# Two buffers for four tiles of a decoder's delta-rule stage, one scaling moved a stage earlier, and a smaller DMA scratch

## The chip, the core and the metric

The kernel runs on one NeuronCore of a Trainium2 chip. Its engines are named as in the profile: PE (TensorE, matrix products and transposes; PEld its weight loads), DVE (VectorE), ACT (ScalarE), POOL (GpSimd) and SP, which here only issues DMAs. A matrix product goes from SBUF into PSUM. The metric is device time in microseconds (us) of one launch, and its median over repeated launches.

## The reference, cut to what matters

Two layers of a decoder over 512 tokens of width 1024. Each layer is a half-step SwiGLU, a mixer, a cross-attention and a second half-step. The mixer's projection feeds three groups of heads: forgetting attention (FoX), block-sparse attention (MoBA) and RWKV-7 time mixing. The change touches the last, whose eight heads of 64 each carry a 64 x 64 state through the tokens:

```
def step(state, inp):
    r_t, w_t, k_t, v_t, kk_t, a_t = inp
    sa = einsum('bhij,bhj->bhi', state, -kk_t)
    state = (state * w_t[:, :, None, :] + sa[..., None] * (kk_t * a_t)[:, :, None, :]
             + v_t[..., None] * k_t[:, :, None, :])
    return state, einsum('bhij,bhj->bhi', state, r_t)
```

Everything else is dense projections, softmax attention and norms, in f32.

## The kernel before, in words

The recurrence is not run token by token. The 512 tokens are cut into 8 chunks of 64, and the 8 heads are taken as 4 head pairs (called 0 to 3 here; two heads fill 128 partitions). A pair goes through six stages, each a function (a generator):

- scaled (L620 on): projections r, k, v become tiles scaled with the cumulated decay. ER holds what is multiplied by the decay since the chunk's start, B what is divided by it, and DC (128 x 8 x 1) the decay to each chunk's end (the copy at L665).
- Gram (`rwkv_gram`): products of B and ER for each chunk (L717) are masked by DVE into G and BN (L721). The strictly triangular blocks of G are stored to DRAM (L726), come back as 16 x 16 blocks in A (L730), and POOL inverts them in 30 dependent steps (helper L282, tiles T and P), copies the result (L742) and stores it again (L746); it comes back as the tiles Tf and Pf (L749).
- rows (`rwkv_rows`): ER is transposed (L763), v is centered (L769) into KV, G times KV goes into KX (L779), B is multiplied by DC, and the result is transposed into BN (L788).
- inverse (`rwkv_inverse`): the 16 x 16 inverses grow to 64 x 64 (L809 reads Tf; L818, L826, L835 and L842 follow and read Pf).
- transitions (`rwkv_transitions`): L857 and L871 make the chunk transitions AR.
- states (`rwkv_states`): 8 chunks in sequence. A step adds L900 and L902 in PSUM, and DVE makes the next state as old state times DC plus that (L906). L920 and L924 to L932 norm and gate the output.

Between these small products stand the long ones: three products for each pair of a 128-column block (L152 to L154, and L948 to L950 for values), since an f32 weight is split into a high part (ACT, L145) and a low part (DVE, L146) after its load (SP, L130). Attention units (L1034 to L1046, with softmax on DVE and ACT, L1016 to L1022) belong to the mixer too.

A list of stages (ORDER, with leads in PRI) gives each instruction a priority. The program that builds the kernel then sets the order on each engine from these priorities, its own estimates of times and the number of buffers of each tile name (RW, RP): an instruction that needs a buffer is put in when the tile before it in that buffer has had its last reader. So an order on the engines is fixed before the kernel runs, and each engine works its list strictly in that order. In the list of stages, the scaling of a pair stands ahead of the states of the pair before it (`s1 ... y0`, `s2 ... y1`, `s3 ... y2`), and those states read that pair's DC and KV. SP's DMAs, weights and small stores alike, also stand in one list.

DC, KV, G and KX have one buffer each; ER, BN and six others have two.

Of the kernel before, what the change touches and what calls it, by code (L numbers as in the profile page):

```python
# [11 lines left out]
ALU = mybir.AluOpType  # L12
# [3 lines left out]
P = 128  # L16
# [32 lines left out]
RPW = {"ts": 0, "sp": 1, "acc": 0, "tx": 1, "ty": 1}  # L49
BPW = {"acc": 0, "sp": 2, "pt": 0, "po": 1}  # L50

RW = {"e": 2, "tk1": 2, "tk2": 2, "zr": 2, "zv": 2, "ER": 2, "zk": 2, "BN": 2}
RP = {"acc": 1, "tx": 1, "ty": 2, "ts": 2, "sp": 2}
WP = {"wraw": 3, "whi": 2, "wlo": 2}

# [60 lines left out]
class Trunk:  # L116
# [585 lines left out]
    def rwkv_gram(self, l, hp, st):  # L702

        nc, rw = self.nc, self.rw
        ps = lambda c=8: self.bank(TAGS["g"], c)
        mm = nc.tensor.matmul
        ER, B = st["ER"], st["B"]

        G = st["G"] = rw.tile([P, 16, 64], F32, name="G", tag="G")

        BN = st["BN"] = rw.tile([P, 8, 4, 64], F32, name="BN", tag="BN")
        for q in range(2):
            pg = [ps(4).rearrange("p c (i t) -> p c i t", i=2) for h in range(2)]
            for c in range(4):
                g, i = 2 * q + c // 2, c % 2
                for h in range(2):
                    mm(pg[h][:, c].rearrange("p i t -> p (i t)"), B[H[h], g, 2 * i:2 * i + 2].rearrange("p a b -> p (a b)"),  # L717
                       ER[H[h], g, 1:3] if i == 0 else ER[H[h], g, 0:4:3], start=True, stop=True)
            for h in range(2):
                for i, dst in ((0, G[:, 8 * h + 4 * q:8 * h + 4 * q + 4]), (1, BN[:, 4 * q:4 * q + 4, 1 + h])):  # L720
                    nc.vector.tensor_tensor(dst, pg[h][:, :, i], self.gmask[:, i:i + 1, :].to_broadcast([P, 4, 64]), op=ALU.mult)  # L721
            yield

        scA, scP, scT = (x[hp % 2] for x in (self.scA, self.scP, self.scT))
        for a in range(2):
            nc.sync.dma_start(scA[a].rearrange("j s t -> s j t"), G[H[a], 1 - a::2])  # L726
        A = rw.tile([64, 16, 16], F32, name="A16", tag="A16")
        for q in range(4):
            d = slice(16 * q, 16 * q + 16)
            nc.sync.dma_start(A[d], scA.rearrange("a j s t -> (a j) s t")[:, d, d])  # L730
        I = rw.tile([64, 16, 16], F32, name="P16", tag="P16")
        tmp = rw.tile([64, 16, 16], F32, name="T16", tag="T16")
        If = I.rearrange("p a b -> p (a b)")
        nc.gpsimd.memset(If, 0.0)
        nc.gpsimd.memset(If[:, 0:256:17], 1.0)
        for u in range(15, 0, -1):
            n = 16 - u
            self.tt("sub", tmp[:, 0:u, 0:n], A[:, 0:u, u:u + 1].to_broadcast([64, u, n]),
                    I[:, u:u + 1, u:16].to_broadcast([64, u, n]), ALU.mult)
            self.tt("sub", I[:, 0:u, u:16], I[:, 0:u, u:16], tmp[:, 0:u, 0:n], ALU.subtract)  # L740
        It = rw.tile([64, 16, 16], F32, name="I16", tag="T16")
        nc.gpsimd.tensor_copy(It, I.rearrange("p a b -> p b a"))  # L742
        for name, sc, src in (("Tf", scT, It), ("Pf", scP, I)):
            for q in range(4):
                d = slice(16 * q, 16 * q + 16)
                nc.sync.dma_start(sc.rearrange("a j s t -> (a j) s t")[:, d, d], src[d])  # L746
            st[name] = rw.tile([P, 8, 64], F32, name=name, tag=name)
            for a in range(2):
                nc.sync.dma_start(st[name][H[a]], sc[a].rearrange("j s t -> s j t"))  # L749
        yield  # L750

    def rwkv_rows(self, l, hp, st):

        nc, rw = self.nc, self.rw
        ps = lambda c=8: self.bank(TAGS["r"], c)
        mm, tr = nc.tensor.matmul, nc.tensor.transpose
        ER, B, G, BN, v = (st[n] for n in ("ER", "B", "G", "BN", "V"))

        KX = st["KX"] = rw.tile([P, 8, 2, 64], F32, name="KX", tag="KX")
        KV = st["KV"] = rw.tile([P, 8, 2, 64], F32, name="KV", tag="KV")  # L760
        pk = ps(4)
        for q in range(4):
            tr(pk[:, q, :], ER[:, q, 0:2].rearrange("p a b -> p (a b)"), self.ident)  # L763
        self.cp("kx", KX[:, :, 0, :].rearrange("p (h q) d -> p q h d", h=2), pk.rearrange("p q (h d) -> p q h d", h=2))
        yield

        pv = ps(4)
        for q in range(4):
            mm(pv[:, q, :], v[:, q * P:(q + 1) * P], self.center, start=True, stop=True)  # L769
        for i in range(2):  # L770
            self.cp("kv", KV[H[i], i::2].rearrange("p q h d -> p q (h d)"), pv[H[i]])
        yield

        px = ps()
        for j in range(8):
            for a in range(2):
                h, i = j // 4, 1 - a
                c = 2 * (j % 4) + i
                mm(px[H[a], j, :], G[H[i], 8 * h + c, :], KV[H[i], c, h, :], start=True, stop=True)  # L779
        self.cp("x", KX[:, :, 1, :], px)  # L780
        yield

        B2 = B.rearrange("p q (i a) b -> p (q i) (a b)", i=2)
        self.tt("B2", B2, B2, st["DC"].to_broadcast([P, 8, P]), ALU.mult)
        for q in range(2):
            pk = ps(4)
            for c in range(4):
                tr(pk[:, c, :], B2[:, 4 * q + c], self.ident)  # L788
            self.cp("bt", BN[:, 4 * q:4 * q + 4, 0:4:3], pk.rearrange("p c (h d) -> p c h d", h=2))
            yield  # L790
# [351 lines left out]
    def mixer_and_xattn(self, l):  # L1142
# [14 lines left out]
        with sb("raw") as raw:  # L1157
# [9 lines left out]
            with sb("rw") as rw0, sb("rwm") as rw1, sb("rwl") as rw2, pp("rp") as rp0, pp("rps") as rp1, pp("rpt") as rp2:  # L1167
                rp = self.tp = TagPool((rp0, rp1, rp2), RP, where=RPW)
                self.rw = at = TagPool((rw0, rw1, rw2), RW, where=LATE)
                w = self.ins['mix_w_in'][l]  # L1170
# [186 lines left out]
```

## Time and profile before

| | |
|---|---|
| median of 3 runs | 2575.36 us (2575.05 to 2586.14) |
| profiled execution | 2590.88 us, span 2589.1 us, 1.8 us around it |
| PE busy | 2497.2 us (96%) |
| DVE, ACT, POOL busy | 1346.6, 846.9, 493.0 us |
| granted TensorE clock, mean | 0.974 of full |
| chain that ended last | PE 86%, DVE 6%, POOL 3%, DMA 2%, ACT 2% |

A busy share of 96% says that PE sets the time, in what it does and in the clock at which it does it; the other engines count only where PE waits for them. PE stands at 2.4 GHz (granted clock 1.00) or 1.2 GHz (0.50). In the timeline rows a bracket gives the idle time of that engine just ahead of the instruction and what ended it.

### The profile page before, as it was taken

What the parts mean: (1) busy time and instruction counts of PE and PEld (TensorE: products, weight loads), DVE (VectorE), ACT (ScalarE), POOL (GpSimd) and SP (SyncE); (2) the same over time, 40 slices, a digit from 0 to 9 for tenths busy, and PEclk for the clock granted to TensorE, in tenths of its full rate; (3) what the DMA queues carried; (4) which work ended last, traced back from release to release, by engine and by line L of the source; (5) the groups of instructions that cost most, each with busy time, mean ns of one, the idle gap of its engine ahead of it and who ended that gap; (6) DMA issues with size and microseconds to landing.
All of it is one profiled execution on the core that took longest, in us unless ns stands there. A gap on an engine that the chain in (4) does not pass through costs nothing.

```text
span 2589.1 us, 35163 instructions
## 1 busy us (share of the span) xinstructions
PE 2497.2 (96%) x13976; PEld 2025.7 (78%) x13976; DVE 1346.6 (52%) x2503; ACT 846.9 (33%) x1337; POOL 493.0 (19%) x610
## 2 busy tenths in 40 slices
PE   8999998899999899999999999999999899999999
PEld 7888876787667788888888888767877677888887
DVE  6444445666755654344444444465666666543444
ACT  4222233233343342222332222333333433422222
POOL 4212120232210122020221211202322110221211
PEclk9999999998889999999999999999978999999999
DMA  4333342221213133333333333422212121333332
GB/s 143 104 98 94 96 130 69 66 59 43 64 34 92 53 96 90 104 93 98 95 94 100 94 98 94 121 75 58 67 34 56 56 78 45 110 98 98 95 95 88
DMA packets 434880, 218.41 MB, mean 84 GB/s; under 512 B 63856, under 2 KB 428828, under 8 KB 434716
## 3 DMA queue, kind: packets, MB, share of 16 engines
q1 hardware_dynamic: 431948, 212.36, 28.9%
q10 hardware_dynamic: 2448, 2.76, 0.3%
q8 instruction: 110, 1.80, 0.3%
q0 software_dynamic: 320, 1.05, 0.1%
q14 instruction: 54, 0.44, 0.1%
HBM read 205.64 MB, written 10.49 MB: 83 GB/s over the span
## 4 chain that ended last, share of the span: by engine, by line
PE 86%; DVE 6%; POOL 3%; DMA 2%; ACT 2%; issue 1%; SPq 1%; POOLq 0%; ACTq 0%; DVEq 0%
PE acc L152 22%; PE acc L154 22%; PE acc L153 22%; PE po L1046 2%; PE sp L1034 1%; POOL P L282 1%; PE pt L1022 1%; PE acc L950 1%; PE acc L948 1%; PE acc L949 1%; POOL T L282 1%; DVE wlo L146 1%; ACT whi L145 1%; PE ts L857 1%; PE ty L717 1%
## 5 line engine op out<-in xcount | busy, mean ns | idle before, releaser
L145 ACT ACTIVATE whi<-wraw 128x1024 fp32r<-128x1024 f32 (+3 forms) x386 | 390.3, 1013 | 1142.0 <-PE acc L153 1043.3
L152 PE MATMUL acc<-xh,whi 128*128 128x512 f32 (+1 forms) x1776 | 699.9, 394 | 21.9 <-DVE p L496 7.3
L154 PE MATMUL acc<-xh,wlo 128*128 128x512 f32 (+1 forms) x1776 | 695.8, 392 | 1.3 <-DVE wlo L146 1.3
L153 PE MATMUL acc<-xl,whi 128*128 128x512 f32 (+1 forms) x1776 | 694.8, 391 | 0.0
L146 DVE TENSOR_TENSOR wlo<-wraw,whi 128x1024 fp32r<-128x1024 f32 (+3 forms) x386 | 540.3, 1401 | 100.3 <-ACT whi L145 91.4
L152 PEld LDWEIGHTS acc<-xh,whi 128*128 128x128 f32 (+1 forms) x1776 | 334.4, 188 | 97.6 <-ACT whi L145 9.1
L154 PEld LDWEIGHTS acc<-xh,wlo 128*128 128x128 f32 (+1 forms) x1776 | 334.2, 188 | 75.5 <-DVE wlo L146 2.6
L153 PEld LDWEIGHTS acc<-xl,whi 128*128 128x128 f32 (+1 forms) x1776 | 334.6, 188 | 69.7
L342 POOL TENSOR_TENSOR up<-up,g 128x512 f32<-128x512 f32 x88 | 118.4, 1346 | 999.2 <-ACT whi L145 901.1
L152 PE MATMUL acc<-th,whi 128*128 128x512 f32 x704 | 274.4, 391 | 1.0 <-ACT whi L145 1.0
L154 PE MATMUL acc<-th,wlo 128*128 128x512 f32 x704 | 275.0, 392 | 0.2
L153 PE MATMUL acc<-tl,whi 128*128 128x512 f32 x704 | 274.0, 389 | 0.0
L295 DVE SCALAR_TENSOR_TENSOR x<-acc,x 128x512 f32<-128x512 f32 x96 | 66.0, 691 | 277.2 <-PE acc L154 277.2
L341 DVE TENSOR_TENSOR up<-acc,rsb 128x512 f32<-128x512 f32 x88 | 60.8, 691 | 278.5 <-PE acc L154 278.5
L338 DVE TENSOR_TENSOR g<-acc,rsb 128x512 f32<-128x512 f32 x88 | 60.8, 691 | 191.0 <-PE acc L154 188.0
L154 PEld LDWEIGHTS acc<-th,wlo 128*128 128x128 f32 x704 | 132.1, 188 | 31.5 <-DVE wlo L146 4.2
L152 PEld LDWEIGHTS acc<-th,whi 128*128 128x128 f32 x704 | 132.2, 188 | 30.5 <-ACT whi L145 4.0
L153 PEld LDWEIGHTS acc<-tl,whi 128*128 128x128 f32 x704 | 132.2, 188 | 27.4
L240 POOL TENSOR_TENSOR sqacc<-sqacc,sq 128x512 f32<-128x512 f32 x48 | 75.4, 1571 | 381.6 <-ACT sq L239 245.9
L346 POOL TENSOR_TENSOR tl<-up,th 128x512 fp32r<-128x512 f32 x88 | 128.5, 1461 | 65.5 <-ACT th L345 65.5
L345 ACT ACTIVATE th<-up 128x512 fp32r<-128x512 f32 x88 | 55.8, 634 | 120.8 <-POOL up L342 120.8
L948 PE MATMUL acc<-whi,xh 128*128 128x256 f32 x256 | 76.9, 300 | 0.7 <-DVE zt L520 0.7
(351 smaller groups left out, 3109.1 us busy)
## 6 DMA issues: line engine op xcount, KB each, us to landing
wraw<-in_ffn_w_in_dram SPq DMA_DIRECT2D x176, 512.0 KB
wraw<-in_ffn_w_out_dram SPq DMA_DIRECT2D x64, 512.0 KB
wraw<-in_mix_w_in_dram SPq DMA_DIRECT2D x52, 512.0 KB
wraw<-in_ffn_w_out_dram SPq DMA_DIRECT2D x32, 384.0 KB
wraw<-in_xattn_w_kv_dram SPq DMA_DIRECT2D x16, 512.0 KB
wraw<-in_mix_w_out_dram SPq DMA_DIRECT2D x16, 384.0 KB
scx<-x SPq DMA_DIRECT2D x16, 256.0 KB
x<-scx SPq DMA_DIRECT2D x16, 256.0 KB
```

Of the source, the lines that this page charges most:

```text
L145: nc.scalar.activation(hv, v, AF.Copy)
L146: nc.vector.tensor_sub(lv, v, f32(hv))
L152: mm(ps, lh, rh, start=start, stop=False)
L153: mm(ps, lh, rl, start=False, stop=False)
L154: mm(ps, ll, rh, start=False, stop=stop)
L240: (nc.vector if m == KC - 1 else nc.gpsimd).tensor_tensor(self.sqacc, self.sqacc, sq, op=ALU.add)
L295: self.nc.vector.scalar_tensor_tensor(xm, ps, coef, xm, op0=ALU.mult, op1=ALU.add)
L338: nc.vector.tensor_tensor(g, pss[0], rsb, op=ALU.mult)
L341: nc.vector.tensor_tensor(up, pss[1], rsb, op=ALU.mult)
L342: nc.gpsimd.tensor_tensor(up, up, g, op=ALU.mult)
L346: nc.gpsimd.tensor_tensor(tl, up, f32(th), op=ALU.subtract)
L948: mm(o, a, wh[:, kk, :], start=k == 0, stop=False)
```

## The change

Four tile names (DC, KV, G, KX) get a second buffer. The multiplication of B by DC goes from the third part of `rwkv_rows` to `rwkv_gram`, behind the Gram products and ahead of the store of G. The DMA scratch that the program reserves is set to 4096 bytes; it was the default.

```diff
-RW = {"e": 2, "tk1": 2, "tk2": 2, "zr": 2, "zv": 2, "ER": 2, "zk": 2, "BN": 2}
+RW = {"e": 2, "tk1": 2, "tk2": 2, "zr": 2, "zv": 2, "ER": 2, "zk": 2, "BN": 2, "DC": 2, "KV": 2, "G": 2, "KX": 2}
@@ rwkv_gram
             yield
 
+        B2 = B.rearrange("p q (i a) b -> p (q i) (a b)", i=2)
+        self.tt("B2", B2, B2, st["DC"].to_broadcast([P, 8, P]), ALU.mult)
+
         scA, scP, scT = (x[hp % 2] for x in (self.scA, self.scP, self.scT))
@@ rwkv_rows
         yield
-
         B2 = B.rearrange("p q (i a) b -> p (q i) (a b)", i=2)
-        self.tt("B2", B2, B2, st["DC"].to_broadcast([P, 8, P]), ALU.mult)
         for q in range(2):
@@ kernel
-    nc = bacc.Bacc("TRN2", target_bir_lowering=False, num_devices=1)
+    nc = bacc.Bacc("TRN2", target_bir_lowering=False, num_devices=1, dynamic_dma_scratch_size=4096)
```

In the changed kernel's order most lines of the mixer's functions are 1 to 3 higher: Tf and Pf come back at L752, the store of G is L729, the state step L907.

DVE, head pair 2 in the first layer, before: the last state steps of pair 1 (L906) and, behind them, the copy that makes pair 2's DC (L665), with softmax instructions (L1018, L1019) around it.

```order
L906 SCALAR_TENSOR_TENSOR tk_4939<-tk_4939,DC,ts 64x64 x2
L277 COPY pT<-pt 128x128
L665 COPY DC<-Dt 128x8
L1018 RECIPROCAL sm<-sm 128x1
L1019 TENSOR_SCALAR p<-p,sm 128x128
```

The same place in the program after the change, pair 2's DC again: it stands among the states of pair 0 (tk_4338).

```order
L907 SCALAR_TENSOR_TENSOR tk_4338<-tk_4338,DC,ts 64x64 x2
L146 TENSOR_TENSOR wlo<-wraw,whi 128x1024
L665 COPY DC<-Dt 128x8
L522 SCALAR_TENSOR_TENSOR zk<-zt,dpar,zk 128x512
L520 TENSOR_TENSOR zt<-acc,rsb 128x512
```

The copy no longer stands behind the last state of the pair before.

POOL, head pair 3 in the first layer, a piece of the difference: T and P are the tiles of the inversion, B<-a,Di makes part of B, B<-B,DC is the multiplication that is moved; left out are the rows between, which are the same but for their lines and numbers.

```order
-L895 MEMSET tk_5805 128x512
-L282 TENSOR_TENSOR zk<-zk,e 128x512
-L282 TENSOR_TENSOR B<-a,Di 128x4x128
-L282 TENSOR_TENSOR T_5537<-A_5531,P_5536 64x15
...
-L282 TENSOR_TENSOR P_5536<-P_5536,T_5537 64x4x12
-L282 TENSOR_TENSOR B<-B,DC 128x1024
-L282 TENSOR_TENSOR T_5537<-A_5531,P_5536 64x3x13
...
+L896 MEMSET tk_5805 128x512
+L282 TENSOR_TENSOR B<-a,Di 128x4x128
+L282 TENSOR_TENSOR B<-B,DC 128x1024
+L282 TENSOR_TENSOR T_5538<-A_5532,P_5537 64x15
```

The multiplication left the middle of the 30 steps and stands ahead of the first.

SP, head pair 3 in the first layer, before: the fetch of A, two weight loads (wraw), the stores of the inverse, the fetches of Tf and Pf.

```order
L730 DMA A_5531<-scA_375 16x16x16 x4
L130 DMA wraw<-in_xattn_w_kv_dram 128x8x128 x2
L746 DMA scP_377<-P_5536 16x16x16 x3
L746 DMA scT_379<-I_5570 16x16x16 x4
L746 DMA scP_377<-P_5536 16x16x16
L749 DMA Tf<-scT_379 64x8x64 x2
L749 DMA Pf<-scP_377 64x8x64 x2
```

After the change, the same:

```order
L733 DMA A_5532<-scA_375 16x16x16 x4
L749 DMA scP_377<-P_5537 16x16x16 x3
L749 DMA scT_379<-I_5571 16x16x16 x4
L749 DMA scP_377<-P_5537 16x16x16
L752 DMA Tf<-scT_379 64x8x64 x2
L130 DMA wraw<-in_xattn_w_kv_dram 128x8x128 x2
L752 DMA Pf<-scP_377 64x8x64 x2
```

The two loads of 512 KB went from behind A's fetch to between Tf and Pf. In the second layer both go ahead of Tf at this pair, where one stood there before; at pair 1 of each layer one load goes ahead of Tf, where none stood.

## Rows read from the trace of the kernel before

**Rows 1.** The page's first part: busy time, share of the span and instructions of each engine.
```profile
PE 2497.2 (96%) x13976; PEld 2025.7 (78%) x13976; DVE 1346.6 (52%) x2503; ACT 846.9 (33%) x1337; POOL 493.0 (19%) x610
```

**Rows 2.** Two stretches, the mixer's RWKV part in the first and the second layer: length, busy time (instructions) of each engine, granted clock, DMA share, GB/s.
```profile
428.00:780.00 352.00, 328.46 (x2785) 258.47 (x2786) 224.70 (x605) 122.67 (x256) 80.65 (x168) 0.91 0.21 55
...
1708.00:2060.00 352.00, 327.86 (x2780) 262.44 (x2781) 222.10 (x601) 122.67 (x255) 79.05 (x167) 0.91 0.22 55
```

**Rows 3.** Who PE waited for between 428 and 780 us: us in total, times, longest us.
```profile
PE ty L809 <- DMA Tf<-scT: 4.1, 3, 2.5
PE ty L788 <- POOL B L282: 3.7, 1, 3.7
PE pt L1022 <- DVE p L1019: 2.6, 2, 2.3
...
PE ty L788 <- POOL Dt L660: 0.4, 1, 0.4
```

**Rows 4.** Timeline, head pair 3 in the first layer, by engine: start us, us, engine, line, operation, operands, shapes, count, idle time ahead.
```profile
687.36 0.49 PE L902 MATMUL ts<-tk,AR 128*128 128x128 f32 x2 [0.29 <-DVE tk L906]
689.46 0.49 PE L902 MATMUL ts<-tk,AR 128*128 128x128 f32 x2 [1.21 <-DVE tk L906]
689.70 0.17 DVE L665 COPY DC<-Dt 128x8 f32<-128x8 f32 x1
693.73 1.89 POOL L282 TENSOR_TENSOR B<-B,DC 128x1024 f32<-128x1024 f32 x1
695.67 1.97 PE L788 MATMUL ty<-ident,B 128*128 128x128 f32 x8 [3.70 <-POOL B L282]
```

**Rows 5.** Timeline, head pair 2 in the first layer (the first five) and in the second: DVE, POOL and PE around the copy of DC.
```profile
623.88 0.29 DVE L1019 TENSOR_SCALAR p<-p,sm 128x128 f32<-128x128 f32 x1
625.34 0.17 DVE L665 COPY DC<-Dt 128x8 f32<-128x8 f32 x1
625.62 2.07 DVE L1019 TENSOR_SCALAR p<-p,sm 128x128 f32<-128x128 f32 x1
625.66 1.90 POOL L282 TENSOR_TENSOR B<-B,DC 128x1024 f32<-128x1024 f32 x1 [1.02 <-DVE sm L1018]
627.83 0.45 PE L1022 MATMUL pt<-ident,p 128*128 128x128 f32 x1 [2.30 <-DVE p L1019]
...
1909.70 2.31 DVE L1019 TENSOR_SCALAR p<-p,sm 128x128 f32<-128x128 f32 x1
...
1912.16 0.45 PE L1022 MATMUL pt<-ident,p 128*128 128x128 f32 x1 [2.59 <-DVE p L1019]
```

**Rows 6.** From the list of PE's waits between 1708 and 2060 us, the state steps.
```profile
PE ts L902 <- DVE tk L906: 2.2, 3, 1.1
```

**Rows 7.** Timeline: from the store of G to L809, which reads Tf. Pair 1 in the first layer, then pair 3 in the first (last Gram products, L809 and L818, which reads Pf), then pair 3 in the second. SPq is SP's queue.
```profile
541.76 1.27 SPq L726 DMA_DIRECT2D scA<-G  x2
568.49 1.28 SPq L749 DMA_DIRECT2D Tf<-scT  x2
571.42 0.29 PE L809 MATMUL ty<-Tf,tk 64*64 64x64 f32 x2 [1.11 <-DMA Tf<-scT]
...
671.80 1.49 PE L717 MATMUL ty<-ER,B 64*128 64x128 f32 x16
708.70 1.97 PE L809 MATMUL ty<-Tf,tk 64*64 64x64 f32 x32
...
711.65 0.86 PE L818 MATMUL ty<-tk,Pf 32*32 32x16 f32 x32
...
1955.38 1.16 PE L717 MATMUL ty<-ER,B 64*128 64x128 f32 x8
1957.02 1.27 SPq L726 DMA_DIRECT2D scA<-G  x2
1986.21 1.15 PE L809 MATMUL ty<-Tf,tk 64*64 64x64 f32 x32
```

**Rows 8.** The fetch of Tf of pair 3 in the first layer and when its bytes end, and the same in the second layer, where a weight load is issued just ahead: SP's timeline, and stretches of 1 us of which the last two columns (DMA share, GB/s) are read; 512 KB is the load.
```profile
702.49 1.27 SPq L749 DMA_DIRECT2D Tf<-scT  x2
706.00:707.00 1.00, 1.00 (x3) 0.43 (x2) 0.69 (x1) 0.00 (x0) 0.00 (x0) 0.50 0.60 135
...
1979.78 0.40 SPq L130 DMA_DIRECT2D wraw<-in_xattn_w_kv_dram  x1
1980.63 1.28 SPq L749 DMA_DIRECT2D Tf<-scT  x2
1982.00:1983.00 1.00, 1.00 (x7) 0.71 (x6) 0.97 (x4) 0.19 (x1) 0.00 (x0) 1.00 1.15 333
...
1985.00:1986.00 1.00, 1.00 (x3) 0.09 (x1) 0.96 (x2) 0.01 (x1) 0.00 (x0) 1.00 0.48 69
```

**Rows 9.** Five stretches at the low clock, columns as in rows 2.
```profile
497.00:504.00 7.00, 6.60 (x41) 5.52 (x42) 1.22 (x6) 0.60 (x1) 0.00 (x0) 0.51 0.62 174
...
627.00:633.00 6.00, 5.17 (x46) 4.20 (x46) 3.25 (x9) 3.16 (x8) 1.03 (x4) 0.50 0.40 77
695.00:712.00 17.00, 16.32 (x77) 8.22 (x79) 7.32 (x20) 4.02 (x8) 3.60 (x9) 0.50 0.24 45
...
1897.00:1917.00 20.00, 17.41 (x96) 14.24 (x97) 10.28 (x29) 6.21 (x17) 7.47 (x22) 0.50 0.19 34
1975.00:1982.00 7.00, 6.32 (x50) 5.26 (x50) 2.56 (x9) 3.60 (x8) 3.17 (x6) 0.51 0.35 59
```

## The prediction

> **What bounds the kernel now.** I read the page's first part, then the list of PE's waits in the stretches where the change works, then the timeline around each wait, and last the clock. PE is busy for 2497.2 us of 2589.1 [rows 1], so a removed wait counts only where PE itself stood, and a slow clock counts everywhere. In the mixer's RWKV part PE idles about 24 us in either layer and its granted clock is 0.91 on average [rows 2]: the waits are small, and the stretches at 1.2 GHz cost more than they do. In the first layer the waits that the edited lines touch are L788 for B (3.7 and 0.4 us), L1022 for a softmax that DVE did late (2.6 in all), the state steps L902, and L809 for the tile Tf, which comes back from DRAM (4.1) [rows 3]. The last is the wait to watch: the change makes everything ahead of it shorter.
>
> **What goes, first layer.** Pair 3's scaling of B waits for DC, and DC for the last state of pair 2 (one buffer). The copy of DC runs at 689.70, POOL is by then inside the inversion, B is scaled from 693.73, and L788 has idled 3.70 us [rows 4]. With two buffers, and the multiplication ahead of the inversion, that is gone: 3.7. The two bare state steps ahead of it idle 0.29 + 1.21 = 1.5 [rows 4]; in the changed order other products stand between them. At pair 1 the 0.4 of L788 goes [rows 3]. At pair 2 DC's copy at 625.34 releases POOL's multiplication at 625.66, and a DVE instruction that takes 0.29 alone takes 2.07 beside it; PE then idles 2.30 at L1022 [rows 5]. I count the 1.8 of stretching. Sum: 3.7 + 1.5 + 0.4 + 1.8 = 7.4 us.
>
> **Second layer.** The same collision takes 2.31 there, 2.0 too much [rows 5], and the state steps give 2.2 [rows 6]. Pair 3's L788 does not wait there. Sum 4.2.
>
> **What is late next: Tf.** From the store of G to L809 pair 1 needs 571.42 - 541.76 = 29.7 us with a wait at its end, so this is what the chain takes [rows 7]. One scaling of B (1.89 [rows 4]) stood inside it and leaves: 27.8. In pair 3 of the first layer L809 starts 708.70 - 673.29 = 35.4 us after the last Gram product (671.80 + 1.49) [rows 7]. Of these, 3.70 + 1.5 were waits, and 17 us from 695 on ran at 1.2 GHz [rows 9], of which 13.7 lie ahead of L809 and give back 6.85 at the high clock: 23.4 of work. In the changed order this stretch gains 11 long products and 18 of L871 and some small ones and loses one gating part; at the spacing of like rows that is 2.7 more (an estimate), so 26.1. The chain from the last product is 27.8 and 0.5 to 1.0 for the store's start (0.5 in the second layer: 1957.02 against 1956.54 [rows 7]), 28.3 to 28.8. New wait: 2.2 to 2.7, I take 2.5. Bounds: 0, if DMA returns faster than in pair 1; 5.0, if the stretch does not win its full clock back. In the second layer, pair 3: 1986.21 - 1956.54 = 29.7, less the state steps' 1.7 of waits and 3.4 of its 6.9 us at the low clock [rows 9], plus 2.0 of products moved in, 26.6; the chain is between 27.1 (its own 1980.63 - 1957.02 to the issue of Tf, and pair 1's 2.9 from there [rows 7, 8], with the start of 0.5) and 28.3. I take 1.2 (0.5 to 1.7).
>
> **SP's list.** The edit moves 512 KB weight loads among the fetches of Tf and Pf. With no load ahead, Tf's bytes end about 4.5 us after its issue (702.49 to 707); with one load ahead, 5.2 to 5.4 (1980.63 to 1986) [rows 8]: 0.7 for one load. Pair 1 gets one load ahead in each layer: 0.7 each (0 to 1.6). In the second layer's pair 3 a second load goes ahead of Tf: 512 KB at the 333 GB/s of that stretch is 1.6 [rows 8]; bounds 0.7 and 2.6, as the load may have the queue to itself or share it. In the first layer's pair 3 both loads stand between Tf and Pf: Pf comes up to 2 x 1.6 = 3.1 later. L818, which reads it, starts 711.65 - 708.70 = 2.95 after L809 [rows 7], and Pf lands about 1.5 after Tf, since its issue follows Tf's by about 1.4 (1.27 of that is Tf's own [rows 8]): 3.1 + 1.5 - 2.95 = 1.7 (0 to 3). Row 8's 0.7 says that a load ahead is only partly in the way. The Trainium skill ("DMA: Bandwidth & Descriptors", section "Queues, rings and completion order") has descriptors on one engine consumed in ring order, so that a small fetch stands behind all bytes queued before it; it speaks against this change, and by it a load is 1.6 each time, which would make the two terms of pair 1 larger by 0.9. This trace shows 0.7, after 0.85 us of head start.
>
> **POOL and DVE.** The multiplication now runs right behind the last making of B, while DVE masks G (L721). A few DVE instructions can be stretched there as at 625.62, ahead of PE: 0.6 in each layer (0 to 1.9, the whole multiplication [rows 5]). The Trainium skill ("SBUF — State Buffer", section "Who interferes with whom") calls the port pair that DVE and GpSimd share an exclusive lock, whose loser waits in full; the 2.07 against 0.29 agrees, and by it the sum would have 1.9 in place of 0.6 where the two meet.
>
> **The end.** The last state steps of pair 3 stand bare in the changed order: they showed up to 1.21 of idle a step [rows 4], I take 1.0 in the first layer and 0.5 in the second (0 to 2.4). The other buffers, G and KX, do not change the order by themselves: nothing. DMA scratch: nothing either; few of the kernel's DMAs are GpSimd's, these stand at its start, and the order is the same with the smaller one. If the scratch had to be recycled it would stall there, and I have no row for it: bounded by zero and by one fetch of 4.5.
>
> **Sum.** First layer: -7.4 + 2.5 + 0.7 + 1.7 + 0.6 + 1.0 = -0.9. Second layer: -4.2 + 1.2 + 1.6 + 0.7 + 0.6 + 0.5 = +0.4. Waits: -0.5 us. The waits trade places. The clock: low stretches stand behind waits, as behind the 3.70 (695 to 712), the 2.30 (627 to 633), behind the second layer's 1912 and in 1975 to 1982 [rows 9]: 17 + 6 + 5 + 7 = 35 us, up to 17 us if they all return to 2.4 GHz. But a stretch like 497 to 504 [rows 9] can follow a wait of 2 us, so the new waits at L809 can bring two of 7, losing 7 together, and a part of 1897 to 1917 may stay: up to 10 net. I take 6. In all 0.5 + 6 = 6.5 us off 2590.9: 2584.4 for a profiled execution. That execution is 0.6% above the median, 2575.4, whose difference I take as a common shift: **2569 us**.
>
> **Rivals.**
> A, the sum as above: 2569 (2560 to 2574).
> B, the clock returns everywhere, and Tf is not late: the wait gains stay at 0.5 plus the 3.7 of new Tf waits and half of SP's 4.7, so 6.5, and the clock gives its 17: 2575.4 - 23.5 = 2552. For it: three of the four stretches stand right behind waits that go. Against: Tf's chain bounds pair 1 already [rows 7], and pair 3 comes to the same bound.
> C, slower: PE gets to L809 earlier and stands there, longer than 2.5 us, because the weight loads are ahead of Tf and Pf. With the loads at the upper price (1.6 in place of 0.7 twice, 2.6 for 1.6, 3 for 1.7) the waits are -0.5 + 1.8 + 1.0 + 1.3 = +3.6, and if each of the four L809 and L818 waits pulls a low stretch of 7 us (3.5 lost each), 14 more while none returns: 2575.4 + 17.6 = 2593. It decides from the point where L809 or L818 waits over 2.5 us in three places. For it: 2 us waits do bring 1.2 GHz [rows 9]; against: 0.7 a load is what row 8 shows.
> D, the change shifts waits only and the clock falls as often as before: 2575. For it, the sum of waits itself is nearly zero.
>
> **How the numbers follow.** A 0.50, B 0.22, C 0.13, D 0.15. The range takes in A and D, C up to half its loss, and B nearly whole: 2551 to 2588; A's own is 2560 to 2574. What this measurement can tell from no change is 0.5%, 12.9 us, so faster means under 2562.5: all of B, and a sixth of A, 0.30. Slower means over 2588.2: nearly all of C, 0.12. Same: 0.58.
>
> **What would show it.** In the changed kernel's waits L788 for B is gone from both layers, and so are the 2 us waits of L1022 at DC's copy; L809 for Tf stands at pair 3 with 1 to 4 us, and L818 for Pf appears in the first layer. The clock is 1.00 from 695 to 705. I would be wrong if L809 in pair 3 does not wait (then the chain is shorter than pair 1's, and B holds), if Pf is not late (then loads do not stand in the way), or if the mixer's granted clock stays at 0.91, with which the time moves by its waits alone.

## The result, and the profile after

The changed kernel takes 2596.23 us (median of 20 runs), the kernel before 2581.86 us (20 runs, on several chips; the 2575.36 of the first table was a median of three). The ratio is 1.0055, 95% interval 1.0041 to 1.0069: slower, by about 14 us. Two of the changed kernel's 20 runs took 7288 and 9471 us and are left out of the ratio; the median of the other 18 is 2595.95 us. The profiled execution of the changed kernel has a span of 2593.6 us.

The page's first part, of the changed kernel, answers [rows 1]: PE is busy 4 us longer, DVE, ACT and POOL a little less.

```profile
PE 2501.0 (96%) x13976; PEld 2029.1 (78%) x13976; DVE 1342.0 (52%) x2503; ACT 846.4 (33%) x1337; POOL 488.0 (19%) x610
```

The same two stretches as [rows 2], of the changed kernel. Idle PE (length less busy) is 22.4 and 26.9 us against 23.5 and 24.1: the waits did trade places.

```profile
428.00:780.00 352.00, 329.65 (x2766) 261.06 (x2765) 221.35 (x605) 122.42 (x254) 77.52 (x168) 0.91 0.21 54
...
1708.00:2060.00 352.00, 325.08 (x2754) 256.87 (x2752) 221.09 (x602) 122.42 (x251) 77.22 (x168) 0.92 0.22 55
```

The list of PE's waits between 428 and 780 us answers [rows 3]. The waits for B at the transposes (L788, here L789) are gone, and several of about 1 us have come.

```profile
PE pt L1023 <- DVE p L1020: 1.7, 1, 1.7
...
PE pt L1023 <- ACT y L916: 1.5, 1, 1.5
PE ty L810 <- DMA Tf<-scT: 1.3, 1, 1.3
...
PE ty L843 <- DVE Pf L279: 0.9, 1, 0.9
PE acc L949 <- DVE zt L520: 0.9, 1, 0.9
...
PE ty L836 <- ACT V L275: 0.8, 1, 0.8
```

The timeline of pair 3 in the first layer of the changed kernel answers [rows 7, 8]: the last Gram product (PE), SP, POOL and PE.

```profile
667.43 1.16 PE L717 MATMUL ty<-ER,B 64*128 64x128 f32 x8
669.08 1.27 SPq L729 DMA_DIRECT2D scA<-G  x2
668.72 1.90 POOL L282 TENSOR_TENSOR B<-B,DC 128x1024 f32<-128x1024 f32 x1 [9.57 <-PE ty L717]
675.85 0.21 POOL L282 TENSOR_TENSOR T<-A,P 64x15 f32<-64x15 f32 x1 [5.23 <-DMA A<-scA]
691.00 1.28 SPq L752 DMA_DIRECT2D Tf<-scT  x2
692.61 5.97 SPq L130 DMA_DIRECT2D wraw<-in_xattn_w_kv_dram  x2
698.69 1.26 SPq L752 DMA_DIRECT2D Pf<-scP  x2
700.05 1.59 PE L810 MATMUL ty<-Tf,tk 64*64 64x64 f32 x32
704.27 0.23 PE L819 MATMUL ty<-tk,Pf 32*32 32x16 f32 x2
```

The multiplication runs in POOL's wait for A and holds up nothing on PE; Tf is issued 9 us ahead of L810, which doesn't wait; Pf is 7.7 us later than Tf and still in time for L819, which starts without idle time.

**Where the 14 us are.** One profile of each can't tell, since the clock differs from execution to execution: the profiled execution of before had a mean granted clock of 0.974, but 23 further runs of it have 0.9777 on average. The changed kernel has 0.9733. If each microsecond at 1.2 GHz did half of one at 2.4, the difference of 0.0044 would be worth 0.0044 x 2590 = 11.4 us. The 23 runs themselves give less: a straight line through their times and clocks has 2.0 us for each 0.001, not 2.6, which makes it 9. Both are estimates: 9 to 11 of the 14 us go with the clock, and 3 to 5 are left for waits and work.

The windows view shows the place. Each row is the stage from pair 3's L809 (L810) to its last gating product, in the first and then the second layer; the columns are those of [rows 2], and 2 x (1 - granted clock) x length gives the time at the low clock. First the kernel before:

```profile
708.70:754.80 46.10, 40.57 (x410) 27.99 (x410) 25.87 (x85) 19.15 (x46) 1.76 (x3) 0.83 0.01 1
1986.20:2036.20 50.00, 42.54 (x418) 29.80 (x418) 27.57 (x89) 20.63 (x50) 1.75 (x2) 0.87 0.01 3
```

The changed kernel:

```profile
700.00:757.90 57.90, 50.85 (x416) 35.20 (x414) 29.09 (x99) 19.36 (x47) 2.36 (x4) 0.71 0.06 15
1985.90:2041.70 55.80, 49.54 (x402) 33.87 (x402) 25.61 (x83) 18.60 (x44) 1.75 (x2) 0.68 0.01 2
```

About as many matmuls (402 to 418), but 34 and 36 us at the low clock instead of 16 and 13. This is not one profile's chance. In the same stage two more profiles with the order of before (e1 and e12, told below) have 13 to 16 us at the low clock and lengths of 46 and 50 us; three more with DC and KV doubled (e2, e4 and e16) have 28 to 55 us and lengths of 55 to 68.

The stretch ahead of it, from pair 1's L809 to pair 3's, is shorter in this pair of profiles. Before:

```profile
571.40:708.70 137.30, 129.09 (x1192) 101.33 (x1192) 90.63 (x220) 44.67 (x94) 36.33 (x76) 0.88 0.23 57
1851.80:1986.20 134.40, 128.26 (x1183) 104.95 (x1183) 86.22 (x216) 43.12 (x91) 34.56 (x75) 0.85 0.24 57
```

After:

```profile
570.00:700.00 130.00, 121.92 (x1198) 98.96 (x1198) 84.86 (x207) 44.39 (x95) 32.91 (x75) 0.95 0.21 53
1856.70:1985.90 129.20, 120.18 (x1210) 98.40 (x1210) 88.33 (x221) 45.01 (x96) 33.09 (x75) 0.95 0.25 59
```

This stretch is 5 to 7 us shorter, as the prediction had hoped, but that is not shown to be the order's doing: in e1, with the order of before, it takes 131.4 and 126.7 us (rows below, under **Clock**), against 130.0 and 129.2 here. The last stage is 6 to 12 us longer, and the prediction had put 1.5 us there for both layers.

### The profile page after: what moved, and what is told of

Its sections match the earlier page's. It is cut to its first block, busy times and chain, and to the rows that moved or that the text cites. A ratio compares the mean times of both kernels' runs of the same rounds, so it can differ in the third digit from the quotient of the medians.

```text
span 2593.6 us, 35175 instructions
## 1 busy us (share of the span) xinstructions
PE 2501.0 (96%) x13976; PEld 2029.1 (78%) x13976; DVE 1342.0 (52%) x2503; ACT 846.4 (33%) x1337; POOL 488.0 (19%) x610
## 4 chain that ended last, share of the span: by engine, by line
PE 87%; DVE 5%; ACT 2%; POOL 2%; DMA 2%; issue 1%; SPq 1%; ACTq 0%; POOLq 0%; DVEq 0%
PE acc L152 22%; PE acc L154 22%; PE acc L153 22%; PE sp L1035 2%; PE po L1047 2%; PE acc L949 1%; PE acc L951 1%; PE pt L1023 1%; PE acc L950 1%; ACT whi L145 1%; PE ts L858 1%; DVE wlo L146 1%; PE ts L901 1%; PE ty L717 1%; POOL P L282 1%
## 5 line engine op out<-in xcount | busy, mean ns | idle before, releaser
L1018 ACT ACTIVATE p<-sp,mx 128x256 f32<-128x256 f32 (+3 forms) x96 | 48.6, 508 | 98.9 <-DVE mx L1017 98.8
```

## The experiments

The theory at the start: the loss is time at the low clock that the new order brings, above all at the end of the mixer. The rivals: the small DMA scratch, the moved multiplication, waits at the full clock. Each ratio is to runs of the kernel before on the same chip; behind it stands the mean granted clock against that of those runs.

**The parts.** e1 has only the last edit of the diff (the scratch), e2 the buffers and the scratch, e3 only the two moved lines of B2, e4 the whole change again.

> Only the DMA scratch of 4096 bytes is new; every engine's order is that of the kernel before. The theory (the loss is a slow clock that the new order brings) expects no change: 0 +- 3 us against the kernel before, and low-clock time as in its runs. The rival (the smaller scratch is what costs) expects the whole loss of the change, +10 to +15 us, with waits for a GpSimd DMA that the kernel before does not have.

> Four buffers and the small scratch; the multiplication of B by DC stays in the rows stage. The theory expects that freeing DC and KV moves the states and the last pair's work, and with it the loss: +8 to +15 us, of which the waits are under 3 us and the rest lies at the low clock. The rival (the moved multiplication and its collision on DVE and POOL cost) expects 0 to -5 us, since the waits of L788 go.

> Only the multiplication of B by DC is moved; one buffer of each, scratch by default. The theory expects about no change, 0 +- 4 us: the L788 wait of 3.7 us at pair 3 becomes a wait of the whole Gram stage for DC. The rival (the moved multiplication is what costs) expects +8 to +15 us.

> The whole change once more, on the chip of the three parts beside it. The theory expects +10 to +16 us against the kernel before, with a mean granted clock lower by 0.003 to 0.005 (each 0.001 is 1.3 us of stretching at half speed, worked out as span x 0.001 / 2 and some more); without the clock's part under 3 us. The rival (slow work or waits at full clock) expects the same clock as before and 10 us more of idle PE.

Measured: e1 2580.65 us, ratio 0.9996 (0.9978 to 1.0014), clock 0.9784 against 0.9777. e2 2595.52 us, 1.0063 (1.0043 to 1.0084), 0.9728. e3 2580.52 us, 0.9995 (0.9977 to 1.0014), 0.9782. e4 2596.12 us, 1.0065 (1.0045 to 1.0086), 0.9732. So scratch and multiplication, each by itself, cost nothing that the runs can tell, and the buffers make the loss. In e2 and e4 the clock is lower by 0.0049 and 0.0045: 12.7 and 11.7 us by the halving, 9.8 and 9.0 at 2.0 us for each 0.001, of losses of 13 to 17. (The 1.3 us for each 0.001 in e4's expectation is too small.)

**One buffer at a time.**

```diff
-... "zk": 2, "BN": 2}
+... "zk": 2, "BN": 2, "DC": 2}      (e5)
+... "zk": 2, "BN": 2, "KV": 2}      (e6)
+... "zk": 2, "BN": 2, "G": 2, "KX": 2}      (e12)
+... "zk": 2, "BN": 2, "DC": 2, "KV": 2}      (e16)
```

All four have the small scratch.

> DC alone gets a second buffer (small scratch, multiplication in the rows stage). The theory: the loss sits in the stretch at the mixer's end in which no long product is left on PE (about 80 us in each layer; 24 us of it at the low clock in three profiles with the old order, 38 to 58 in three with the new one). By the order this kernel keeps that stretch as it was, with pair 3's transposes of B in it, so 0 +- 4 us and about 24 us of low clock there. The rival (freeing DC is what costs, since it moves the states) expects +8 to +15 us.

> KV alone gets a second buffer. The theory expects 0 +- 4 us and about 24 us of low clock in the last stretch of each layer, as that stretch holds nearly the same products as before; the rival (KV's buffer is what costs) expects +8 to +15 us.

> G and KX alone get a second buffer, with the small scratch; the order of every engine is that of the kernel before. The theory (the order makes the loss) expects 0 +- 4 us and about 14 us of low clock from pair 3's L809 to its gating. The rival (where tiles stand in SBUF) expects +8 us or more.

> DC and KV doubled, G and KX single, small scratch: the order of every engine is that of e2 (+13 us). The theory (the order makes the loss) expects +10 to +16 us; the rival (the place of tiles in SBUF, G and KX doubled, makes part of it) expects +4 to +8 us.

Measured: e5 2589.19 us, 1.0018 (0.9998 to 1.0037), between the two expectations and not told from no change. e6 2580.02 us, 0.9989 (0.9970 to 1.0007); the end of its second layer has 40 us at the low clock instead of the 24 expected, and yet the kernel is not slower. e12 2586.10 us, 1.0026 (1.0006 to 1.0046), though its order is that of the kernel before. Its mean clock is lower (0.9760 against 0.9778), but its profile can't show where, since it is of its fastest run (2575.39 us). Whether these 6 us are the place of tiles or chance stays open. e16 2598.93 us, 1.0067 (1.0046 to 1.0089): with G and KX single the loss is whole, so they are not needed for it. It needs DC and KV together. A reading that no run tests: only then do a pair's scaling and its rows both get free of the states before.

**Long products later.** The theory in its first form said that the lack of long products at the end brings the low clock. e7 (on the change) and e8 (on the kernel before) move a projection:

```diff
-ORDER = ("... f11 f00 i2 mq V3 t2 s3 g3 r3 f20 f10 i3 y2 ..."
+ORDER = ("... f11 f00 i2 V3 t2 s3 g3 r3 f20 f10 mq i3 y2 ..."
```

> The whole change, and in the list of stages the projection mq (long products) goes from ahead of V3 to ahead of i3, so that the stretch without long products at the mixer's end is shorter (by the order some 5 to 7 us less of matrix work in it). The theory expects less low clock there, 20 to 35 us in each layer, and 5 to 12 us less than the change: +2 to +10 us against the kernel before. The rival (the low clock at the end belongs to the last states and their wait of 5 us at L925, not to the lack of long products) expects the same 38 to 58 us there, and a new low stretch where mq stood: +14 us or more.

> The kernel before with the same move of mq. The theory expects a gain, 0 to -8 us, with less than 24 us of low clock at the end of each layer; the rival expects no gain or a loss of 0 to +8 us, since a second stretch without long products appears ahead of the last (by the order 39 us of matrix work).

Measured: e7 2604.35 us, 1.0081 (1.0056 to 1.0106); e8 2589.40 us, 1.0017 (0.9999 to 1.0036). The stretch without long products at the mixer's end got shorter (67 to 73 us in e7 against 80 to 85 in the change's profile), and its low clock fell, as the theory said: 33 and 24 us in e7 against 37 and 44, and 17 and 13 in e8 against 34 and 24. But a second such stretch opened where mq had stood, with 20 and 7 us at the low clock in e7 and 24 and 27 in e8, and no time came back. In time the rival held. It is not enough to put long products near the end.

**Which pair's freedom.** Both are the change with two tags; pair 1 alone (e9), or pair 3 alone (e10), takes the second tag:

```diff
-name="DC", tag="DC")
+name="DC", tag="DCb" if hp == 1 else "DC")      (e10: hp == 3)
-name="KV", tag="KV")
+name="KV", tag="KVb" if hp == 1 else "KV")      (e10: hp == 3)
```

> The change, but of DC and KV only pair 1 uses the second buffer: pair 1 is free of pair 0's states, pair 3's scaling waits for pair 2's states as in the kernel before. The theory (the loss is the freedom of the last pair: its inverse starts earlier, attention products run out and its last states stand bare, at the low clock) expects the stage from pair 3's L810 to its gating to have about 14 us of low clock in each layer, as with the old order (13 to 15 in three profiles), and the time at 0 +- 4 us against the kernel before. The rival (the freedom of the earlier pairs, or any double buffer of DC and KV together, costs) expects about 37 us there, as with the change, and +8 to +15 us.

> The change, but of DC and KV only pair 3 uses the second buffer: it is free of pair 2's states, the pairs before it wait as in the kernel before. The theory expects the whole loss or more, +10 to +20 us, with 30 to 50 us of low clock from pair 3's L810 to its gating in each layer. The rival expects 0 +- 4 us.

Measured: e10 2599.51 us, 1.0080 (1.0055 to 1.0106), clock 0.9702 against 0.9783: the freedom of pair 3 alone is enough for the whole loss, some 20 us, most of it clock (16 us at 2.0 for each 0.001, 21 by the halving). Its last stage has 49 and 22 us at the low clock, where 30 to 50 were expected in each layer. e9 2597.03 us, 1.0065 (1.0046 to 1.0084), against the theory's 0. It does not show what pair 1's freedom costs, since in its second layer the last states are packed as in the change. By its order pair 3's states have 12 us of matrix work from the first step to the last in the first layer, as before, and 9 in the second, as with the change (an estimate, at the spacing of like rows). So one and the same execution has both kinds of last stage:

```profile
699.90:751.20 51.30, 43.84 (x413) 30.82 (x414) 25.69 (x84) 18.97 (x45) 2.25 (x3) 0.84 0.02 4
1986.00:2043.60 57.60, 50.09 (x401) 35.31 (x402) 24.22 (x81) 17.94 (x43) 1.19 (x1) 0.65 0.04 8
```

16 us at the low clock, and 40. Both layers together, the stage takes 108.9 us, against 96.1 before. By the clock (0.9745 against 0.9783) 8 to 10 of its 16 us are explained; the others are not.

**The wait at the end, filled.**

```diff
         pyt = ps(1)[:, 0, :]
+        for _ in range(8 if hp == 3 else 0):
+            mm(pyt, g2[:, 0, :], self.gs[0], start=True, stop=True)
```

> The change, and ahead of the transposes L925 of pair 3's states PE gets 8 products of 512 columns whose results nobody reads; they stand in the wait for DVE (5.3 us, longer than they take at the high clock), as do the two products of the gate. If the wait is what keeps the clock low behind it, the low stretch around it (741 to 762 us) gets shorter by 5 to 10 us in each layer and the time falls by 3 to 8 us against the change, +6 to +11 us against the kernel before. The rival (the clock there is set by the small products ahead of it, and the products only add work) expects the same 20 us at the low clock and the time of the change or up to 5 us more.

Measured: 2613.78 us, 1.0126 (1.0105 to 1.0147), some 17 us over the change. The added products (x16 in the row) and the first gating product behind them, in e11:

```profile
746.86 8.54 PE L925 MATMUL ts<-gs,g 128*128 128x512 f32 x16
755.24 1.02 PE L933 MATMUL ts<-gs,g 128*128 128x512 f32 x2
```

The products took 8.5 us (8.3 in the second layer), more than the wait of 5.3, and the gating behind them runs at the high clock: 1.02 us for what takes 1.91 in the change (row of L931 below). The stage has 27 and 29 us at the low clock, 7 less than the change's profile in either layer, and about its length (59.3 and 57.0 us against 57.9 and 55.8). So neither side held: the clock came back in part, as the theory said, but the time did not fall, and it rose by more than the rival allowed. The profiled execution is 12 us longer than the change's, and 10 of these lie behind the second layer's gating; why is open.

**The last states themselves.** The theory in its second form: pair 3's states want attention products between them. The timeline shows what is meant. First PE in e1 (the order before), the last state steps: L902 comes every 2 to 3 us, with L1034 between.

```profile
727.93 0.49 PE L902 MATMUL ts<-tk,AR 128*128 128x128 f32 x2
...
728.74 1.13 PE L1034 MATMUL sp<-mk,mq 64*128 64x512 f32 x4
729.92 0.44 PE L902 MATMUL ts<-tk,AR 128*128 128x128 f32 x2
...
735.06 0.74 PE L902 MATMUL ts<-tk,AR 128*128 128x128 f32 x2
735.73 1.22 PE L1034 MATMUL sp<-mk,mq 64*128 64x256 f32 x2
...
741.31 1.09 PE L924 MATMUL ts<-ident,tk 128*128 128x128 f32 x4 [4.14 <-DVE tk L920]
```

In the changed kernel the last steps (L903) have only L901 between them, the wait is longer, and the gating runs at the low clock (two products of L931 take 1.91 us).

```profile
745.15 0.74 PE L903 MATMUL ts<-tk,AR 128*128 128x128 f32 x2
745.68 0.95 PE L901 MATMUL ts<-KV,BN 128*128 128x64 f32 x4
746.56 0.79 PE L903 MATMUL ts<-tk,AR 128*128 128x128 f32 x2
747.14 0.96 PE L901 MATMUL ts<-KV,BN 128*128 128x64 f32 x4
748.04 0.79 PE L903 MATMUL ts<-tk,AR 128*128 128x128 f32 x2
754.09 1.09 PE L925 MATMUL ts<-ident,tk 128*128 128x128 f32 x4 [5.26 <-DVE tk L921]
754.97 1.91 PE L931 MATMUL ts<-gs,g 128*128 128x512 f32 x2
```

e13 spreads them again with all buffers kept, e14 is the control, e15 packs them in the kernel before, without any buffer:

```diff
-... mk y1 f11 f00 i2 mq V3 t2 s3 g3 r3 f20 f10 i3 y2 t3 f30 f21 y3 ...
+... mk y1 f00 i2 mq V3 t2 s3 g3 r3 f11 f20 f10 i3 y2 t3 f30 f21 y3 ...      (e13, e14)
+... mk y1 f11 f00 i2 mq V3 t2 s3 g3 r3 f20 f10 f21 i3 y2 t3 f30 y3 ...      (e15)
```

> The whole change, and in the list of stages the attention unit f11 goes from ahead of f00 to behind r3, so that pair 3's states get as much work between them as in the kernel before (by the order 11 to 12 us of matrix work from the first to the last, 9 with the change). The theory expects 13 to 20 us of low clock from pair 3's L810 to its gating in each layer and a time of -6 to +6 us against the kernel before. The rival (the buffers' cost does not hang on those states) expects 30 us or more of low clock there and +10 to +16 us.

> The same move of f11 in the kernel before, as a control: the states of pair 3 keep their 11 to 12 us of work. The theory expects 0 +- 5 us and about 14 us of low clock from pair 3's L809 to its gating; the rival, that f11 late helps any order, expects -5 us or less.

> The kernel before with single buffers; in the list of stages the attention unit f21 goes ahead of i3, so that pair 3's inverse and states look like those of the change (by the order 7 and 9 us of matrix work from the first state step to the last; 9 and 9 with the change, 11 and 12 before), while the pairs ahead of it stay about as they were. The theory (little attention work left for the last states is what brings the low clock) expects 25 to 50 us of low clock from pair 3's L809 to its gating in each layer and +6 to +15 us. The rival (the buffers, or the pairs before, are the cause) expects 13 to 20 us there and 0 +- 4 us.

Measured: e13 2572.81 us, 0.9975 (0.9951 to 0.9998), clock 0.9813 against 0.9778. e14 2561.14 us, 0.9928 (0.9903 to 0.9953), clock 0.9857. e15 2590.42 us, 1.0035 (1.0009 to 1.0062), clock 0.9758. The last stage of e13, first and second layer:

```profile
692.60:739.00 46.40, 39.95 (x419) 27.09 (x418) 29.01 (x97) 19.72 (x48) 2.24 (x3) 0.89 0.01 3
1968.60:2022.80 54.20, 48.67 (x411) 34.52 (x410) 25.34 (x83) 18.02 (x44) 0.91 (x1) 0.69 0.01 3
```

and of e15:

```profile
706.40:765.50 59.10, 52.73 (x409) 36.36 (x410) 25.65 (x84) 18.69 (x44) 1.75 (x2) 0.64 0.03 7
1994.90:2044.20 49.30, 41.33 (x408) 28.67 (x407) 25.32 (x83) 18.56 (x44) 1.25 (x2) 0.83 0.03 6
```

e15 makes 8 us of loss and, in the layer where the states got tightest, 43 us of low clock, with single buffers: a packed tail can cost without the change. Its second layer, packed about as in the change, has only 17, below its expectation. e13 took 23 us from the change, and the first layer's stage went to 10 us of low clock, but the second's stayed at 34, outside its expectation. And the control takes 19 us from the kernel before, where no tail was packed: a late f11 helps either order. If the two gains add, the restored tail has some 4 of e13's 23 us, which the intervals do not tell from nothing.

One more run speaks to this. e5 (DC doubled alone) has a tail at least as packed as e15's, in both layers. Its last steps in the first layer, with the same wait and the same slow gating as in the change:

```profile
739.55 0.95 PE L900 MATMUL ts<-KV,BN 128*128 128x64 f32 x4
740.44 0.79 PE L902 MATMUL ts<-tk,AR 128*128 128x128 f32 x2
747.98 1.09 PE L924 MATMUL ts<-ident,tk 128*128 128x128 f32 x4 [5.27 <-DVE tk L920]
748.86 1.91 PE L930 MATMUL ts<-gs,g 128*128 128x512 f32 x2
```

Its last stage has 27 and 24 us at the low clock, but is no longer than before (98.2 us over both layers, 96.1 before), and the kernel loses at most 10 us (ratio 1.0018, at most 1.0037). So a packed tail has more low clock in most stages that have one, but by itself it costs little in e5 and 8 us (2 to 16) in e15. It is shown to be a part of the cause; that it is the whole 14 us is not shown.

**A combination.** e17 is e14 with KV doubled and the small scratch.

> KV doubled (e6, -2 us) and f11 moved (e14, -19 us) in the kernel before. If both are independent: -18 to -24 us against the kernel before. The rival (a double buffer and a late f11 take from the same waits) expects -8 to -16 us.

Measured: 2568.65 us, 0.9948 (0.9927 to 0.9970): no better than e14, as the rival said. e14, an attention unit listed later and no buffer added, is the fastest of all and beats both kernels.

## Why the prediction was wrong

**Waits.** The sum, -0.5 us, came out nearly right: all idle time of PE in the two RWKV stretches went from 47.7 to 49.3 us (lengths less busy, above). That was luck, since waits that were foreseen did not come and others came in their place.
- Right: L788's waits for B went, and so did the collision. L1020 takes 0.29 us behind the copy of DC at that place (now pair 3's), where no multiplication of B runs any more. But the wait of 2.30 became 1.73, not 0.5: late next was ACT, which copies the state (1.55 us) ahead of the softmax that PE needs.

The timeline of the changed kernel at that place, DVE, ACT and PE:

```profile
622.47 1.55 ACT L275 ACTIVATE tk<-ts 64x256 f32<-64x256 f32 x4 [0.23 <-DVE tk L907]
622.49 0.15 DVE L665 COPY DC<-Dt 128x8 f32<-128x8 f32 x1
622.61 0.29 DVE L1020 TENSOR_SCALAR p<-p,sm 128x128 f32<-128x128 f32 x1
624.04 0.37 ACT L1018 ACTIVATE p<-sp,mx 128x128 f32<-128x128 f32 x1
625.08 0.33 PE L1023 MATMUL pt<-ident,p 128*128 128x128 f32 x1 [1.73 <-DVE p L1020]
```

- Wrong: the new wait for Tf at pair 3 (2.5 and 1.2 us). The store of G to the issue of Tf takes 691.00 - 669.08 = 21.9 us there, while pair 1, from which I took the chain, has 568.49 - 541.76 = 26.7 with 1.9 of B in it [rows 7]. No step of pair 3's inversion takes over 0.4 us here, while some in pair 1 took 0.8 to 1.3, and the chain is 3 us shorter than I took it. And PE needs 31.5 us from the last Gram product to L810 (668.59 to 700.05), not 26.1: 5 us more. So Tf is early, not late.
- Wrong: Pf behind two loads (1.7 us). It is issued 7.7 us after Tf, later than the 4.5 I took (3.1 for the two loads' bytes and 1.4), since SP itself stands 5.2 us between the two loads, waiting for DVE. But Tf is early, L819 starts 4.2 us after L810, not 2.95, and so 5.6 us after Pf's issue, and nothing waits. In the second layer, too, L810 does not wait for a Tf behind two loads.
- The smaller terms were about right or cost nothing: pair 1's wait for Tf, with a load ahead, grew from 1.11 to 1.34 us and from 1.04 to 1.73 (0.7 each was taken), and beside the moved multiplication a DVE instruction of 0.69 us took 1.87 at pair 3, for which PE did not wait.
- Not foreseen: many waits of 0.4 to 1.9 us for ACT and DVE (L836, L843, L949, L1023 for y) that came with the new order.

**Clock.** This is the term that failed: "I take 6" back, with a whole of up to 17. It was a loss of 9 to 11 (0.9777 to 0.9733 in the means of runs). The sign that the prediction named for this came true: the mixer's granted clock stayed at 0.91 and 0.92 (rows above), and from 695 to 705 us it was 0.83, not 1.00. Two steps of the term were wrong. I took each low stretch as the price of the wait ahead of it, so that a wait that goes gives its stretch back. But low stretches stand where PE hardly waits, too: in the changed kernel it is busy for 29.20 of these 30 us, with a longest wait of 0.8, at 0.72 of the clock.

```profile
700.00:730.00 30.00, 29.20 (x268) 20.01 (x268) 12.77 (x38) 6.89 (x18) 0.53 (x1) 0.72 0.11 28
```

Between pairs 1 and 3 that seemed to hold: low time there falls from 33 and 40 us to 13 and 13 in the two profiles. But the last stage, to which I gave 1.0 and 0.5 us of bare steps, took 41 us more low clock over both layers and is 17.6 us longer. And I read the low stretches off one profile whose clock (0.974) was well under the kernel's mean (0.978): 137 us of low clock in it, against 2 x (1 - 0.9777) x 2580 = 115 in the mean. I called the 0.6% (15.5 us) that this execution lay over the median a common shift. It was two things: the median of three was 6.5 us under that of 20 runs, and the other 9 us are nearly all clock (0.974 against 0.9777 is 7 to 10). In e1, the same order in another execution, the stretch from pair 1 to pair 3 has 0.92 in both layers, 21 and 20 us at the low clock: two thirds of what went there between the two profiles was not the order's.

```profile
567.20:698.60 131.40, 122.59 (x1191) 97.23 (x1191) 90.70 (x220) 44.67 (x94) 36.10 (x76) 0.92 0.23 58
1840.30:1967.00 126.70, 120.49 (x1183) 98.46 (x1183) 86.22 (x216) 43.10 (x91) 34.68 (x75) 0.92 0.25 61
```

**The rivals.** C had the sign and the mechanism of low clock, with 2593 on the scale of 2575, 18 us; but not its place: it put the low clock behind waits at L809 and L818, which did not come. The sign for B, no wait at pair 3's L809, came true without B's gain. D, no change, was 14 us off on that scale. The range, 2551 to 2588, left out the result. Of the 27 us between 2569 and 2596, 6.5 are the median of three that the sum started from; the other 21 are a gain of 6 that was a loss of 14.

**Scratch, G and KX.** Scratch at nothing is shown by e1. That G and KX are nothing is shown for the order, and e16 shows that the loss does not need them; what e12 adds by itself stays open.

**What stays open.** What makes the rest of the loss, beyond the packed tail. 12 us lie between e13 and e14, whose tails are alike by their order. In their profiles the last stage takes the same time over both layers (100.6 and 100.3 us), while the stretch from pair 1's L809 to pair 3's takes 256.4 us in e13 and 243.1 in e14 (258.1 in e1): there the late f11 gains with single buffers, and hardly with doubled ones. Open also is what in the packed stretch makes the clock fall: in e11 a filled wait brought the gating back to the high clock, but not the kernel's time.

## What to carry to other kernels

A second buffer does not only remove a wait: with a planner that fixes the order, it lets work run ahead, and what is left behind can end up alone at the end. Look at the last stage of the new order first, for what stands between the dependent steps there, and price it at the clock that such stretches have in the trace. And take the clock's share from several executions, since one profile here lay 9 us over its kernel's median, nearly all of it clock.

## What was not expected of the hardware

The time of one kernel varies mostly with the granted clock: over 23 runs of the kernel before, between 2573.83 and 2593.84 us, the mean clock goes from 0.982 to 0.971, and 0.001 of clock goes with about 2 us (correlation -0.92). Two kernels with the same order (e1 and the kernel before) have profiles with 85 and 137 us at 1.2 GHz.
